# Key selection of a sparse-attention layer: two of six query blocks counted by a compare with sum on VectorE, and masks written into the score tiles

## Chip, core and metric

The kernel runs on one NeuronCore of a Trainium2 chip. A core has five engines that run side by side, each with its own queue of instructions: TensorE (matrix products into PSUM), VectorE, ScalarE and GpSimd (element-wise work and reductions), and SyncE, which here only starts DMAs. The metric is the device time of one execution in microseconds (us), median of several runs; lower is better.

## What is computed

One layer of a decoder trunk over 1024 positions of width 1024, in float32: a half-step SwiGLU feed-forward, then two token mixers side by side (sparse attention A and stick-breaking attention B), each gated and merged, then a second half-step feed-forward. The change lies in the selection of keys for the sparse attention. For each query, an indexer scores all keys up to its own position, and only the 256 best take part in the attention:

```python
dots = einsum('bthd,bsd->bths', qi, k_idx)
score = einsum('bths,bth->bts', relu(dots), wi)
score = where(causal, score, -inf)
_, idx = lax.top_k(score, top_k)            # top_k = 256
valid = idx <= t_pos
# logits of q_a with the chosen keys, softmax, product with the chosen values
```

Queries are handled in blocks of 128. Block i sees (i + 1) x 128 keys. Blocks 0 and 1 have at most 256 keys, so all of them are chosen; blocks 2 to 7 need a selection. What the selection hands on is a mask per block: 0 for a chosen key, -1e30 for any other, to be added to the logits.

## The kernel before

**Stages.** The first feed-forward comes first (to about 640 us in the profile), then the projections of the mixers, the mixers themselves (about 700 to 1425 us), then the output projection and the second feed-forward. Within the mixers the kernel is a set of Python generators. Each `yield` names an engine and the tiles or marks that the next piece of work needs; a planner (`Weave`, lines 94 to 242) holds a model of when each engine is free and each tile ready, and always continues the generator whose next piece can start earliest. Ties go by a rank (0 first), then by the time at which a piece became ready plus an optional slack (the `2.0` in `yield ACT, cand, score[i], 2.0`). The order that comes out is fixed when the program is built: on the chip each engine works through its queue in that order.

**Generators around the change.**

- `indexer` and `dot_out` (1603 to 1642) build the score tiles `score[i]`, float32, 128 queries x (i + 1) x 128 keys, named `u` in the profile, in the order 5, 4, 2, 7, 6, 3. `score_out` sets keys after the query's position to -3e38.
- `topk` (1225 to 1323) makes the selection, once for the group (5, 4, 2) and once for (7, 6, 3). Both run at the same time as everything below.
- `sticks`, `sigmoids`, `stick` (1691 to 1736) and `values` (1792 to 1819) are the stick-breaking attention: a product into PSUM (`psz`), two sigmoids on ScalarE, a scan (line 1701, tile `left`) and a multiplication (1704) on VectorE, transposes on TensorE (`pstT`), a copy on ScalarE (1748) and a subtraction on VectorE (1750) that split the result into a high and a low part (`pt`), and the product with the values (`psy`), which `y_out` stores (`yl`, `yh`).
- `fillers` (1197 to 1222) has the lowest rank: projections (`psf`) of queries, keys, values and gates, which TensorE takes whenever nothing else is ready. Once "gates" is marked, the next fillers are the output projections in `outputs` (2061), first `psob`. These need the marks "gates" and "o", the operands `ybh` and `ybl` in the place of the tiles that the gate projections read, and the mark "c".
- `values` marks "o" at its end, waits for "top0" and "top1", closes the memory of the selection (`chosen.close()`, `keep.close()`: the score tiles among it), and starts `sparse` (1831), which reuses that memory for the loads `uvraw` and marks "c".
- `logits`, `soft`, `latent_values` (1873 to 1967) are the sparse attention proper. Logits (`psL`) start at the mark "sparse", after the last stick; for blocks 5 and 4 the masks need "top0", for 7, 6 and 3 "top1".

**How the selection works.** The 256th largest score is found bit by bit. `count(0.0)` counts the scores that are at least zero, which gives `sig`: +1 if the threshold is positive, -1 if not. Then `by_sign` goes through 31 bits from the highest down. For each bit VectorE sets the bit in a candidate (`cand`, line 1257), ScalarE computes for each block of the group the sign of `sig * score + cand` with the sum over the keys (line 1260; the instruction is followed by a read of its accumulator), VectorE compares the three sums with `thr` (1264, `m`) and keeps the bit or not (1265). `cand` carries the sign bit, so the sum tells how many scores lie above the candidate. Candidates of the next bit need the test of this one; a group's bits are a chain through both engines.

After the bits a few small operations and one more `count(fix)` round the threshold (lines 1271 to 1294). Then each block gets its mask, one block after another: sign of the score against the threshold on ScalarE (1305, `gt`), equality (1308), a running sum for ties (1311, `cum`), the difference (1314), the mask in bfloat16 (1318), and a DMA from GpSimd's queue (1321) to the buffer `bd` in DRAM. The three temporary tiles come from a ring of three (`x2`). The mask is written over the tile `cum`, which is given back only when that DMA has landed; the next block's pass needs all three tiles.

Of the kernel before, what the change touches and what calls it, by code (L numbers as in the profile page):

```python
# [10 lines left out]
F32 = mybir.dt.float32  # L11
F32R = mybir.dt.float32r
I32 = mybir.dt.int32
BF16 = mybir.dt.bfloat16
# [3 lines left out]
ALU = mybir.AluOpType  # L18
# [5 lines left out]
P = 128  # L24
# [221 lines left out]
def trunk(ctx, tc, x, positions, g_ffn1, w1_gate, w1_up, w1_down, g_mix, w_in, g_cq, w_uq_a, w_q_idx,  # L246
# [781 lines left out]
    with ctxf, fp as fpool, psm as psum, tc.manual_schedule(  # L1028
# [193 lines left out]
            mark("gates", *outs)  # L1222


        def topk(group, gi):
            n = len(group)

# [18 lines left out]
            nc.vector.tensor_scalar(kth, sig, TOPK - 0.5, 0.5, op0=ALU.mult, op1=ALU.add)  # L1246
            for b, i in enumerate(group):
                c = slice(b, b + 1)
                nc.vector.tensor_scalar(thr[:, c], sig[:, c], 2 * TOPK - 1.0 - (i + 1) * P, 1.0, op0=ALU.mult, op1=ALU.add)


            def by_sign(bits):

                yield DVE
                nc.vector.tensor_scalar(T, T, -2147483648, None, op0=ALU.bitwise_or)
                for bit in bits:
                    nc.vector.tensor_scalar(cand, T, 1 << bit, None, op0=ALU.bitwise_or)  # L1257
                    for b, i in enumerate(group):
                        yield ACT, cand, score[i], 2.0
                        nc.scalar.activation(junks[1][:, 0:(i + 1) * P], score[i], AF.Sign,  # L1260
                                             scale=sig[:, b:b + 1], bias=cand.bitcast(F32)[:, b:b + 1],
                                             accum_out=cnt[:, b:b + 1])
                    yield DVE, cnt
                    nc.vector.tensor_tensor(m, cnt, thr, op=ALU.is_ge)
                    nc.vector.scalar_tensor_tensor(T, m, bit, T, op0=ALU.logical_shift_left, op1=ALU.bitwise_or)
                nc.vector.tensor_scalar(T, T, 0x7FFFFFFF, None, op0=ALU.bitwise_and)

            nc.vector.memset(T, 0)
            yield from by_sign(range(30, -1, -1))

            lo16, hi16 = tl("lo16", I32), tl("hi16", I32)
            nc.vector.tensor_scalar(lo16, T, 0xFFFF, None, op0=ALU.bitwise_and)
# [24 lines left out]
            for b, i in enumerate(group):  # L1297
                nk = (i + 1) * P
                x2 = here["x2"]
                yield ACT, (x2, 3), fix  # L1300
                tiles = [x2(n_) for n_ in ("eq", "cum", "gt")]
                eq, cum, gt = (t[:, 0:nk] for t in tiles)
                c = slice(b, b + 1)

                nc.scalar.activation(gt, score[i], AF.Sign, bias=fix[:, c], accum_out=cnt[:, c])
                yield DVE, gt

                nc.vector.tensor_scalar(eq, gt, 0.0, STEP, op0=ALU.is_equal, op1=ALU.mult)
                nc.vector.tensor_scalar(rem[:, c], cnt[:, c], -0.5 * STEP, (TOPK - 0.5 * nk) * STEP, op0=ALU.mult, op1=ALU.add)
                yield DVE  # L1310
                nc.vector.tensor_tensor_scan(cum, eq, eq, 0.0, op0=ALU.add, op1=ALU.bypass)
                yield DVE
                nc.vector.scalar_tensor_tensor(rem[:, c], cum[:, nk - 1:nk], 0.5, rem[:, c], op0=ALU.mult, op1=ALU.add)
                nc.vector.tensor_sub(eq, cum, gt)
                give(tiles[2])
                bias = tiles[1].bitcast(BF16)[:, 0:nk]
                yield DVE
                nc.vector.tensor_scalar(bias, eq, rem[:, c], NEG, op0=ALU.is_gt, op1=ALU.mult)
                give(tiles[0])
                yield POOL, tiles[1]  # L1320
                put_low(bd[:, boff[i]:boff[i] + nk], bias)
                give(tiles[1])
            mark(f"top{gi}", bd)

        def heads():
# [923 lines left out]
```

## Time and profile before

| | |
|---|---|
| Time, median of 3 runs (lowest to highest) | 2187.26 us (2185.01 to 2187.8) |
| The profiled execution | 2190.85 us, span 2189.1 us |
| Busy in the span: TensorE / VectorE / ScalarE / GpSimd | 2139.3 / 1550.2 / 1117.2 / 888.5 us |
| Instructions | 30352 |
| Signs of the bit search (line 1260) | 186, 183.4 us of ScalarE, from 808.5 to 1196.3 us, and as many accumulator reads |

Times in the profile are from the start of the span. PE is TensorE's matrix products, PEld its weight loads, DVE is VectorE, ACT ScalarE, POOL GpSimd, SP SyncE. A line number is the line of the kernel; work done in a helper stands under the helper's line, so tiles tell more than lines there. In a group, the number after x is its count, then come the busy time, the mean of one in ns, and the idle time of the engine just before, with what ended it. The clock is the share of TensorE's full clock that was granted. A busy TensorE is not a TensorE at its peak: matmuls overlap in the records.

### The profile page before, as it was taken

To read this page: it belongs to the slowest core of one execution; us is meant where nothing else is said; L and a number is where in the kernel's file an instruction comes from. 1 tells how busy PE (TensorE), PEld (TensorE's weight loads), DVE (VectorE), ACT (ScalarE), POOL (GpSimd) and SP (SyncE) were. 2 spreads that over 40 slices of the span, in tenths; PEclk is the share of its full clock that TensorE was granted. 3 is DMA by queue.
4 is the path that set the end of the run, shared out by engine and by line. 5 is a ranking of instruction groups with operands and counts; after the bars stand their busy time and mean duration, and the time that the engine had idled before them with its cause. 6 is when DMAs were issued, how large, how long until landed. Compare 5 with 4: busy or idle time off the path is not lost.

```text
span 2189.1 us, 30352 instructions
## 1 busy us (share of the span) xinstructions
PE 2139.3 (98%) x10308; PEld 1782.2 (81%) x10308; DVE 1550.2 (71%) x2562; ACT 1117.2 (51%) x2185; POOL 888.5 (41%) x718
## 2 busy tenths in 40 slices
PE   7999999999999999999999899999999999999999
PEld 6888888887889988788888688878888888888887
DVE  7766767678874698677788888853674655678685
ACT  6433333334454358999988565534433232233443
POOL 5555555522354444211111232255465554552223
PEclk9999999999999999999999899999999999999999
DMA  5587878496675353655554433566132332349755
GB/s 156 143 248 209 252 200 255 159 318 230 218 198 169 121 144 127 238 143 176 155 174 140 151 124 107 191 219 219 58 125 92 99 109 92 116 167 322 234 176 188
DMA packets 269053, 381.00 MB, mean 174 GB/s; under 512 B 23265, under 2 KB 157041, under 8 KB 268897
## 3 DMA queue, kind: packets, MB, share of 16 engines
q1 hardware_dynamic: 256384, 339.17, 49.4%
q0 software_dynamic: 12512, 39.89, 5.1%
q8 instruction: 81, 1.33, 0.3%
q14 instruction: 76, 0.61, 0.1%
HBM read 259.94 MB, written 119.05 MB: 173 GB/s over the span
## 4 chain that ended last, share of the span: by engine, by line
PE 53%; issue 9%; DVE 9%; ACT 4%; DMA 4%; POOL 2%; SPq 0%; POOLq 0%; DVEq 0%; ACTq 0%
PE p L737 4%; PE p L738 4%; PE p L736 4%; ACT junka L1260 2%; PE pa L499 2%; PE pa L498 2%; PE pa L497 2%; PE pc L498 2%; PE pc L499 2%; PE pc L497 2%; PE pd L498 2%; PE pd L499 2%; PE pd L497 2%; PE psf L308 2%; PE psf L309 2%
## 5 line engine op out<-in xcount | busy, mean ns | idle before, releaser
L1260 ACT ACTIVATE junka<-u,cand,sig 128x768 bf16<-128x768 f32 (+4 forms) x186 | 183.4, 986 | 7.9 <-DVE cand L1257 6.1
L859 ACT ACTIVATE swh<-swr 128x512 fp32r<-128x512 f32 x48 | 30.2, 629 | 116.8 <-PE pc L499 51.4
L1701 DVE TENSOR_TENSOR_SCAN left<-left 128x640 f32<-128x640 f32 (+3 forms) x64 | 86.1, 1348 | 3.1 <-ACT left L1693 2.9
L1194 POOL DMA_DIRECT2D gd<-evg x32 | 18.0, 563 | 140.9 <-ACT evg L1189 124.6
L860 DVE TENSOR_TENSOR swr<-swr,swh 128x512 f32<-128x512 f32 x48 | 42.0, 875 | 38.1 <-ACT swh L859 35.2
L1750 DVE TENSOR_TENSOR pt<-pstT,pt 128x512 fp32r<-128x512 f32 (+1 forms) x96 | 51.0, 550 | 24.3 <-ACT pt L1748 23.7
L640 ACT ACTIVATE b0u<-b0u 128x512 f32<-128x512 f32 x20 | 12.7, 633 | 99.0 <-DVE b0u L520 83.0
L1750 DVE TENSOR_TENSOR pt<-pspT,pt 128x512 fp32r<-128x512 f32 x72 | 46.4, 683 | 19.0 <-ACT pt L1748 18.9
L1748 ACT ACTIVATE pt<-pspT 128x512 fp32r<-128x512 f32 x72 | 39.6, 596 | 33.6 <-PE pspT L1960 33.5
L1881 ACT ACTIVATE e<-e,nm 128x768 f32<-128x768 f32 (+7 forms) x64 | 49.4, 775 | 11.4 <-DVE nm L1876 10.9
L737 PE MATMUL p<-aT,aS 128*128 128x512 f32 x132 | 51.9, 394 | 2.4 <-DVE aT L378 2.3
L1614 DVE SCALAR_TENSOR_TENSOR u<-relu,WI,u 128x512 f32<-128x512 f32 (+1 forms) x70 | 50.2, 739 | 5.3 <-ACT relu L1607 4.3
L1869 DVE CUSTOM_DVE_ANT_0 e<-psL,bias 128x512 f32<-128x512 f32 (+3 forms) x96 | 49.7, 549 | 5.1 <-PE psL L1906 5.1
L737 PE MATMUL p<-bT,bS 128*128 128x512 f32 x132 | 51.5, 390 | 0.4 <-DVE bT L378 0.4
L1704 DVE TENSOR_TENSOR sa<-sa,left 128x639 f32<-128x639 f32 (+3 forms) x64 | 48.0, 753 | 4.0 <-ACT sa L1695 0.2
L738 PE MATMUL p<-aT,aS 128*128 128x512 f32 x132 | 50.7, 389 | 0.0
L738 PE MATMUL p<-bT,bS 128*128 128x512 f32 x132 | 50.4, 389 | 0.0
L1607 ACT ACTIVATE relu<-psdot 128x512 f32<-128x512 f32 (+1 forms) x80 | 39.7, 522 | 20.7 <-DVE u L1614 9.2
L1960 PE MATMUL pspT<-ident,e 128*128 128x128 f32 x288 | 41.7, 287 | 7.8 <-DVE e L1884 7.7
L1748 ACT ACTIVATE pt<-pstT 128x512 fp32r<-128x512 f32 (+1 forms) x96 | 46.3, 502 | 3.7 <-PE pstT L1804 3.6
L1960 PEld LDWEIGHTS pspT<-ident,e 128*128 128x128 f32 x288 | 36.2, 148 | 14.0 <-DVE e L1884 9.0
L1695 ACT ACTIVATE sa<-psz 128x512 f32<-128x512 f32 (+2 forms) x96 | 47.0, 509 | 0.1
(3038 smaller groups left out, 8257.1 us busy)
## 6 DMA issues: line engine op xcount, KB each, us to landing
aw<-in_w_down_dram SPq DMA_DIRECT2D x33, 512.0 KB, 5.2
bw<-in_w_down_dram SPq DMA_DIRECT2D x33, 512.0 KB, 5.0
swr<-in_w_in_dram SPq DMA_DIRECT2D x48, 256.0 KB, 6.2
a0r<-in_w_gate_dram SPq DMA_DIRECT2D x22, 512.0 KB, 7.5
a1r<-in_w_up_dram SPq DMA_DIRECT2D x22, 512.0 KB, 7.4
b0r<-in_w_gate_dram SPq DMA_DIRECT2D x22, 512.0 KB, 4.0
b1r<-in_w_up_dram SPq DMA_DIRECT2D x22, 512.0 KB, 3.8
x<-in_x_dram SPq DMA_DIRECT2D x16, 512.0 KB, 6.9
```

Source lines behind the costliest of these rows:

```text
L497: nc.tensor.matmul(ps, a[:, c], b[k][:, HI], start=start and k == 0, stop=False, skip_group_check=True)
L498: nc.tensor.matmul(ps, a[:, c], b[k][:, LO], start=False, stop=False, skip_group_check=True)
L499: ins = nc.tensor.matmul(ps, a[:, l], b[k][:, HI], start=False, stop=k == 3, skip_group_check=True)
L736: nc.tensor.matmul(ps[q][m], S[:, h], T[:, HI], start=p == 0, stop=False)
L737: nc.tensor.matmul(ps[q][m], S[:, h], T[:, LO], start=False, stop=False)
L738: nc.tensor.matmul(ps[q][m], S[:, l], T[:, HI], start=False, stop=p == last)
L1260: nc.scalar.activation(junks[1][:, 0:(i + 1) * P], score[i], AF.Sign, scale=sig[:, b:b + 1], bias=cand.bitcast(F32)[:, b:b + 1], accum_out ...
L1614: nc.vector.scalar_tensor_tensor(ac, r, wv, ac, op0=ALU.mult, op1=ALU.add)
L1701: nc.vector.tensor_tensor_scan(back, back, back, 1.0, op0=ALU.mult, op1=ALU.bypass)
L1748: nc.scalar.activation(pt[:, off:512], tp[:, off:512], AF.Copy)
L1750: nc.vector.tensor_sub(pt[:, 512 + off:1024], tp[:, off:512], f32(pt[:, off:512]))
L1960: nc.tensor.transpose(tp[:, q * P:(q + 1) * P], E[n + q][:, j * P:(j + 1) * P], ident)
```

## The change

Blocks 2 and 3, one in each group, are counted in another way. For these two, `flip` multiplies the score tile in place by `-sig` before the bits and again after them (which restores it). In each bit their count is then a comparison on VectorE, `score < cand`, with its sum over the keys, in the form that `count` has already; the other two blocks of a group keep their sign on ScalarE. The comparison of a group is issued ahead of its signs. `thr` for these blocks is set for a plain count in place of a sum of signs. In the mask passes of all six blocks the temporary tile `cum` is given back once it has been read, and the mask is written into the block's own score tile, from which the DMA to `bd` reads it.

```diff
+        compared = (3, 2)
+
         def topk(group, gi):
...
-                nc.vector.tensor_scalar(thr[:, c], sig[:, c], 2 * TOPK - 1.0 - (i + 1) * P, 1.0, op0=ALU.mult, op1=ALU.add)
+                nk = (i + 1) * P
+                if i in compared:
+                    nc.vector.tensor_scalar(thr[:, c], sig[:, c], TOPK - 0.5 * (nk + 1), 0.5 * (nk + 1), op0=ALU.mult, op1=ALU.add)
+                else:
+                    nc.vector.tensor_scalar(thr[:, c], sig[:, c], 2 * TOPK - 1.0 - nk, 1.0, op0=ALU.mult, op1=ALU.add)
+
+            def flip():
+
+                for b, i in enumerate(group):
+                    if i in compared:
+                        yield DVE
+                        nc.vector.tensor_scalar(score[i], score[i], sig[:, b:b + 1], -1.0, op0=ALU.mult, op1=ALU.mult)
...
-                    for b, i in enumerate(group):
+                    for b, i in sorted(enumerate(group), key=lambda bi: bi[1] not in compared):
+                        if i in compared:
+                            yield DVE, cand, score[i], 2.0
+                            nc.vector.tensor_scalar(junks[0][:, 0:(i + 1) * P], score[i], cand.bitcast(F32)[:, b:b + 1], 0.0,
+                                                    op0=ALU.is_lt, op1=ALU.add, accum_out=cnt[:, b:b + 1])
+                            continue
                         yield ACT, cand, score[i], 2.0
                         nc.scalar.activation(junks[1][:, 0:(i + 1) * P], score[i], AF.Sign,
...
             nc.vector.memset(T, 0)
+            yield from flip()
             yield from by_sign(range(30, -1, -1))
+            yield from flip()
...
                 nc.vector.tensor_sub(eq, cum, gt)
                 give(tiles[2])
-                bias = tiles[1].bitcast(BF16)[:, 0:nk]
+                give(tiles[1])
+                bias = score[i].bitcast(BF16)[:, 0:nk]
                 yield DVE
                 nc.vector.tensor_scalar(bias, eq, rem[:, c], NEG, op0=ALU.is_gt, op1=ALU.mult)
                 give(tiles[0])
-                yield POOL, tiles[1]
+                yield POOL, score[i]
                 put_low(bd[:, boff[i]:boff[i] + nk], bias)
-                give(tiles[1])
```

## The prediction

> **What bounds the kernel now.** I read the page's busy table first, then the busy time in stretches of 50 us, then the groups and single rows around the key selection. The columns of the stretches are: from:to, length, then busy time (instructions) of TensorE, its weight loads, VectorE, ScalarE and GpSimd, the granted clock, the DMA share and GB/s.
>
> ```profile
> PE 2139.3 (98%) x10308; PEld 1782.2 (81%) x10308; DVE 1550.2 (71%) x2562; ACT 1117.2 (51%) x2185; POOL 888.5 (41%) x718
> ...
> 800.00:850.00 50.00, 47.67 (x250) 40.93 (x249) 44.37 (x86) 38.85 (x80) 20.50 (x21) 0.97 0.33 107
> ...
> 1000.00:1050.00 50.00, 49.56 (x264) 40.44 (x264) 36.94 (x74) 49.77 (x116) 4.40 (x9) 1.00 0.61 170
> 1050.00:1100.00 50.00, 49.48 (x258) 39.93 (x257) 38.16 (x66) 49.21 (x110) 7.59 (x14) 1.00 0.55 161
> ...
> 1200.00:1250.00 50.00, 39.70 (x169) 29.66 (x168) 42.41 (x117) 23.90 (x45) 14.44 (x17) 0.83 0.46 159
> 1250.00:1300.00 50.00, 49.52 (x280) 42.56 (x279) 40.59 (x153) 30.93 (x79) 17.28 (x17) 1.00 0.41 130
> ...
> 1950.00:2000.00 50.00, 50.00 (x223) 41.40 (x222) 44.98 (x58) 19.44 (x35) 19.35 (x12) 1.00 0.84 291
> ...
> 800.00:1205.00 405.00, 397.23 (x2084) 328.12 (x2083) 320.38 (x636) 373.33 (x810) 83.17 (x120) 1.00 0.53 162
> ...
> 1205.00:1253.00 48.00, 37.88 (x162) 28.39 (x161) 40.25 (x118) 24.37 (x45) 11.60 (x14) 0.82 0.46 158
> ```
>
> TensorE is busy for 98% of the span. The change touches no matmul, so it can win only time in which TensorE stands idle or runs at a lowered clock. ScalarE is full from 1000 to 1100 (49.8 and 49.2 of 50), yet TensorE is 99% busy there too: the planner fills it with the gate projections (`fillers`). So a shorter ScalarE queue gives no direct gain in that stage. The one large hole lies behind it: from 1205 to 1253 TensorE is busy 37.9 of 48 us, at a clock of 0.82. That is 10.1 us idle and about 0.18 x 37.9 = 6.8 us of slow clock: **16.9 us is what can be won here**.
>
> Why the hole is there is read from single rows (columns: start, length, engine, line; in brackets the idle time before and what ended it), from three one-line summaries, and from the landing line of the mask buffer `bd`.
>
> ```profile
> L1189 ACT ACTIVATE evg<-psf x32: 574/596/677, 936.8 to 1215.3; 128x512 f32<-128x512 f32 x32
> ...
> L1701 DVE TENSOR_TENSOR_SCAN left<-left x64: 416/1349/2292, 912.6 to 1188.4; 128x640 f32<-128x640 f32 x8, 128x768 f32<-128x768 f32 x8, 128x896 f32<-128x896 f32 x8, 128x1024 f32<-128x1024 f32 x8
> ...
> 1206.65 0.59 ACT L1757 ACTIVATE yl<-psy 64x512 f32<-64x512 f32 x1 [6.69 <-DMA ybld<-yl]
> ...
> 1208.37 0.32 SPq L2068 DMA_DIRECT2D ybh<-ybhd  x1
> ...
> 1210.62 1.14 ACT L1305 ACTIVATE gt<-u,fix 128x1024 f16<-128x1024 f32 x1
> ...
> 1220.36 0.47 PE L1960 MATMUL pspT<-ident,e 128*128 128x128 f32 x1 [4.42 <-DVE e L1884]
> ...
> 1221.01 0.32 SPq L2069 DMA_DIRECT2D ybl<-ybld  x1
> ...
> 1224.35 1.03 ACT L1305 ACTIVATE gt<-u,fix 128x896 f16<-128x896 f32 x1
> ...
> 1228.52 2.02 DVE L1311 TENSOR_TENSOR_SCAN cum<-eq 128x896 f16<-128x896 f16 x1 [2.56 <-DMA bd<-cum]
> ...
> 1237.43 0.71 ACT L1305 ACTIVATE gt<-u,fix 128x512 f16<-128x512 f32 x1
> ...
> 1245.08 0.57 POOL L1321 DMA_DIRECT2D bd<-cum  x1 [7.44 <-DVE ri L1883]
> ...
> 1247.40 0.98 POOL L1840 MEMSET uvraw<- 128x512 f32 x2 [1.74 <-DMA bd<-cum]
> ...
> 1250.79 0.39 PE L308 MATMUL psob<-ybh,ob0h 128*128 128x512 f32 x1
> ...
> DMA to landing us min/median/max: 1.9/2.6/5.4
> ```
>
> The gate projections end at about 1215 (last eviction of `psf` at 1215.3). The next filler, the projection `psob`, begins only at 1250.8. In between TensorE has the attention work alone and waits for VectorE (4.42 us before 1220.36). `psob` needs the mark "c", which `values` gives after "top0" and "top1", once the tiles of the selection can be closed. The `uvraw` memset at 1247.4, the first work on the freed memory, waits for the last mask DMA. So **the selection of the second group (blocks 7, 6, 3) decides when the hole ends**: its last sign is at 1196.3 (below), its three mask passes begin at 1210.6, 1224.4 and 1237.4, and its last mask leaves at 1245.1. The stick-breaking work was done by then: last scan at 1188.4, last `yl` at 1206.7.
>
> **The change, part by part.** First the price of what moves: signs on ScalarE with their accumulator reads (groups between 900 and 1200; busy, mean ns), then compares with sum on VectorE.
>
> ```profile
> L1260 ACT ACTIVATE junka<-u,cand,sig x186: 692/1016/1376, 808.5 to 1196.3; 128x768 bf16<-128x768 f32 x31, 128x640 bf16<-128x640 f32 x31, 128x384 bf16<-128x384 f32 x31, 128x1024 bf16<-128x1024 f32 x31
> ...
> L1260 ACT ACTIVATION_READ_ACCUMULATOR junka<-u,cand,sig 128x1 f32 x138 | 29.2, 211 | 0.0
> ...
> L1260 ACT ACTIVATE junka<-u,cand,sig 128x512 bf16<-128x512 f32 x29 | 23.9, 825 | 0.3
> ...
> L1260 ACT ACTIVATE junka<-u,cand,sig 128x384 bf16<-128x384 f32 x18 | 13.2, 734 | 0.1
> ...
> L1237 DVE TENSOR_SCALAR_CACHE_REDUCE junkv<-u x6: 544/878/1208, 800.2 to 873.6; 128x768 bf16<-128x768 f32 x1, 128x640 bf16<-128x640 f32 x1, 128x384 bf16<-128x384 f32 x1, 128x1024 bf16<-128x1024 f32 x1
> ...
> L1237 DVE TENSOR_SCALAR_CACHE_REDUCE junkv<-u,fix 128x768 bf16<-128x768 f32 x1 | 1.0, 1005 | 0.0
> ...
> L1237 DVE TENSOR_SCALAR_CACHE_REDUCE junkv<-u,fix 128x384 bf16<-128x384 f32 x1 | 0.6, 606 | 0.0
> ...
> 1207.88 0.73 DVE L1237 TENSOR_SCALAR_CACHE_REDUCE junkv<-u,fix 128x512 bf16<-128x512 f32 x1
> 1208.54 0.07 DVE L1237 DVE_READ_ACCUMULATOR junkv<-u,fix 128x1 f32 x1
> ...
> L1884 DVE TENSOR_SCALAR e<-e,ri 128x768 f32<-128x768 f32 x8 | 5.5, 685 | 0.3
> ```
>
> 1. *Signs removed.* 31 bits for block 2 (384 keys) and 31 for block 3 (512 keys): 31 x (0.734 + 0.211) + 31 x (0.825 + 0.211) = 29.3 + 32.1 = 61.4 us of ScalarE. From 800 to 1205 ScalarE falls from 373.3 to about 312 of 405 us (77%).
>
> 2. *Compares added.* 31 x (0.606 + 0.07) + 31 x (0.73 + 0.07) = 21.0 + 24.8 = 45.8 us of VectorE. The changed line has the same operation with the same shapes as L1237, so I take those rows. The four flips are VectorE scalings in place; each is shorter than the 768-element one of L1884 (0.685 us), so 2.7 us at most, once per block before and after all bits. VectorE rises from 320.4 to 320.4 + 45.8 + 2.7 = 369 of 405 us (91%).
>
> The 768-element pair bounds this from below: a scaling without a sum takes 0.685 us where the compare with sum takes 1.005 us, so at the scaling's pace the 45.8 us would be some 31. The Trainium skill ("VectorE: DVE Perf Modes", the perf-mode tier table) gives fp32 `tensor_scalar` from SBUF two elements a cycle; by its breakdown of 150 cycles and half a cycle per element an estimate for both kinds of compare together is 26 us, before their reads. The row with the sum, 1.005 us for 768, shows no such rate, and the row decides.
>
> 3. *What the bits gain.* The second group's 31 bits run from about 875 (its first counts end at 874) to 1196.3, 10.4 us a bit, of which its own three signs (median 1.016) and reads (0.211) are only some 3.7 us; the rest is standing in a full ScalarE queue three times a bit. One of three stands goes away; the compare takes one on VectorE instead, issued ahead of the two signs. If a third of a bit is saved and a quarter of that is given back, a bit is 2.6 us shorter and the second group ends 31 x 2.6 = 80 us earlier. To be out of the way at 1206.7 (`yl`, end of the sticks) it needs to end some 35 us earlier. I take that as reached, since the margin is double; the bounds are nothing and 80.
>
> 4. *Masks into the score tiles.* `cum` is no longer held by the DMA. The visible wait for that is 2.56 us (VectorE before 1228.5), and the planner spaces the passes 13 us apart because it reckons with the landing. On their own the masks would end some 2 x 2.6 to 2 x 5.4 us earlier, 5 to 11 us, by the landing line. Behind step 3 this is off the path. The DMA itself, its bytes and its place in GpSimd's queue stay; the score tile is held to its landing instead, and it was held to the same mark before.
>
> 5. *What is late next.* With "top1" early, "c" follows the end of the values, about 1213 as I estimate it (the `yl` of 1206.65 and its way into DRAM). Then `psob` waits for its operands: the `ybh`/`ybl` loads take the place of `h2`, so they start only as the gate projections end; the last is issued at 1221.0 and lands some 5 us later. So `psob` can begin at about 1226 instead of 1250.8, and the hole shrinks from 1215-1251 to 1215-1226, 11 of 36 us: 16.9 x 11/36 = 5.2 us stay and **11.7 us are won**. Three mask passes less in that stretch relieve VectorE, which had 40.3 of 48 us there; I count nothing for it.
>
> 6. *What VectorE costs the stage before.* The end of the sticks is now set by ScalarE (92% from 800 to 1205) and would be set by VectorE at 91%. The highest share of VectorE in any stretch is 44.98 of 50, 90%. At 90% the 369 us need 410 us, 5 later than now; at 95% they need 388, 17 earlier. I take 0 to 1 us lost, since the fillers cover TensorE on either side.
>
> Sum: -11.7 + 0.7 = **-11.0 us**. The profiled execution took 2190.85 us, 1.75 us around its span of 2189.1, so it would be 2179.9. It lies 3.6 us above the median of the runs, 2187.26, so I put the time at 2176.3, rounded **2176**.
>
> **The rivals.** Two waits of VectorE over 800 to 1205 matter for them (us, times, longest):
>
> ```profile
> DVE m L1264 <- ACT junka L1260: 25.4, 23, 2.6
> DVE pt L1750 <- ACT pt L1748: 23.7, 28, 2.2
> ```
>
> *A. The whole hole closes.* ScalarE's relief ends the sticks before the gate projections are used up, and these fill TensorE until `psob` is ready. Condition: VectorE keeps up at about 95%. For it: those waits for ScalarE, 49 us, shrink when ScalarE has room. Against it: no stretch shows VectorE above 90%. Time: nearly all of 16.9 us and some of the 2.3 us idle from 800 to 850, about -18 us: 2169.
>
> *B. The bits come no faster.* The compare stands as long in VectorE's queue as the sign stood in ScalarE's, and the second sign is issued only after it. Then "top1" stays near 1245 but for the DMA wait, 3 us or so are won and VectorE gives them back: 2186. For it: VectorE is at 91%. Against it: two of three stands remain on an engine that has gone from 92% to 77%.
>
> *C. Slower: VectorE becomes the bound.* A compare of 0.6 to 0.8 us stands in front of the scans (L1701) and of the split subtraction L1750, whose `pt` frees the two transpose banks; and the test `m` still waits for the last sign with all this behind it. If half of the 45.8 us lengthens the stage because the 49 us of waits stay, the sticks end at 1228 with the fillers gone at about 1215; 23 us are lost and step 5's 11.7 won: 2187 + 11 = 2198. It decides from the point at which the sticks end 12 us later than now; with the whole 45.8 us it would be 2221. The Trainium skill ("TensorE: Matmul & The Clock Gate", engine queue depths) says that ScalarE's and VectorE's queues are strictly first in, first out. The 25.4 us of waits before `m` agree with that as far as a wait can; by that rule alone C's mechanism holds, and only its size is open.
>
> **How the numbers follow.** Forecast 0.45 (own range 2170 to 2182), A 0.20, B 0.15, C 0.20. Within 0.2%, 4.4 us, which is about what a measurement of this kernel can tell from no change, lie B and little else. So faster 0.65, same 0.16, slower 0.19. The range goes from 2165 (A with a few us more, the lower bound on the compares) to 2195 (B and the milder half of C); about 0.2 is left out, mostly C.
>
> **What would show it.** Right: 124 signs at the sign's line and 62 compares of 0.61 and 0.73 us; ScalarE near 310 and VectorE near 365 us from 800 to 1205; the last sign before 1165; `uvraw` waiting for no mask DMA; `psob` from about 1226; TensorE above 44 of 50 us from 1200 to 1250 with a clock above 0.9. Wrong: a last stick scan after 1200 (C), a last sign after 1185 (B), no gap between the gates and `psob` (A), or new idle time of TensorE from 800 to 1200.

## The result and the profile after

| | before | after |
|---|---|---|
| Time, median of 7 runs each (lowest to highest) | 2187.8 us (2185.01 to 2193.09) | 2176.9 us (2172.76 to 2181.68) |
| Ratio to before, 95% interval | 1 | 0.9945 (0.9928 to 0.9962) |
| The profiled execution | 2190.85 us, span 2189.1 us | 2175.96 us, span 2174.2 us |

The changed kernel is 0.55% faster; the forecast was 2176. In the table of experiments below, one run of first_before (2421.5 us) and one of yl_on_pool (9050.66 us) were slow ones: they count in the medians of their rows and not in the ratios. The page of the changed kernel, the line of busy times:

```profile
PE 2133.8 (98%) x10308; PEld 1779.0 (82%) x10308; DVE 1583.0 (73%) x2690; ACT 1072.8 (49%) x2061; POOL 885.4 (41%) x716
```

The same stretches of the changed kernel as were shown of before, with the same columns (length, busy time of TensorE, weight loads, VectorE, ScalarE, GpSimd, then the clock):

```profile
950.00:1000.00 50.00, 50.00 (x263) 41.06 (x262) 46.18 (x95) 46.70 (x102) 7.75 (x14) 1.00 0.57 165
1000.00:1050.00 50.00, 50.00 (x275) 41.05 (x274) 46.18 (x98) 49.22 (x108) 4.41 (x8) 1.00 0.58 157
1050.00:1100.00 50.00, 50.00 (x255) 41.09 (x255) 45.57 (x102) 40.21 (x86) 8.39 (x15) 1.00 0.57 170
...
1200.00:1250.00 50.00, 43.57 (x222) 34.40 (x222) 43.91 (x139) 31.27 (x62) 13.39 (x17) 0.97 0.50 172
1250.00:1300.00 50.00, 47.78 (x266) 40.70 (x265) 44.03 (x151) 31.74 (x78) 11.76 (x11) 0.97 0.30 95
...
800.00:1205.00 405.00, 400.15 (x2099) 330.75 (x2097) 362.25 (x783) 333.92 (x693) 84.89 (x124) 1.00 0.54 168
...
1205.00:1253.00 48.00, 42.41 (x222) 33.93 (x223) 41.95 (x135) 28.81 (x58) 12.35 (x17) 0.96 0.42 142
```

TensorE from 1205 to 1253 went from 37.88 us at a clock of 0.82 to 42.41 us at 0.96. What is lost there is the length less busy time times clock: 48 - 42.41 x 0.96 = 7.3 us, against 16.9. So 9.6 us were won where 11.7 were forecast. From 800 to 1205 TensorE is busy 2.9 us more than before, with VectorE at 92% in the stretches from 950 to 1050. From 1250 to 1300 a little is given back.

What answers to the single rows of before (summaries by line, then rows of the timeline: start, length, engine, line; in brackets the idle time before and what ended it):

```profile
L1278 ACT ACTIVATE junka<-u,cand,sig x124: 912/1116/1349, 811.4 to 1160.4; 128x768 bf16<-128x768 f32 x31, 128x640 bf16<-128x640 f32 x31, 128x1024 bf16<-128x1024 f32 x31, 128x896 bf16<-128x896 f32 x31
...
L1274 DVE TENSOR_SCALAR_CACHE_REDUCE junkv<-u,cand x62: 585/666/747, 812.5 to 1160.2; 128x384 bf16<-128x384 f32 x31, 128x512 bf16<-128x512 f32 x31
...
L1262 DVE TENSOR_SCALAR u<-u,sig x4: 415/447/481, 804.8 to 1168.9; 128x384 f32<-128x384 f32 x2, 128x512 f32<-128x512 f32 x2
...
L1721 DVE TENSOR_TENSOR_SCAN left<-left x64: 391/1346/2285, 915.8 to 1187.4; 128x640 f32<-128x640 f32 x8, 128x768 f32<-128x768 f32 x8, 128x896 f32<-128x896 f32 x8, 128x1024 f32<-128x1024 f32 x8
...
L1189 ACT ACTIVATE evg<-psf x32: 573/598/712, 925.0 to 1203.9; 128x512 f32<-128x512 f32 x32
```

```profile
1181.87 1.14 ACT L1325 ACTIVATE gt<-u,fix 128x1024 f16<-128x1024 f32 x1
...
1199.98 0.71 ACT L1325 ACTIVATE gt<-u,fix 128x512 f16<-128x512 f32 x1
...
1207.35 0.54 POOL L1342 DMA_DIRECT2D bd<-u  x1
...
1207.50 0.58 PE L1925 MATMUL psL<-kkh,qs 128*128 128x256 f32 x1 [3.33 <-DVE mx L1889]
...
1213.62 0.32 SPq L2089 DMA_DIRECT2D ybl<-ybld  x1
...
1213.68 0.99 POOL L1860 MEMSET uvraw<- 128x512 f32 x2 [5.26 <-DMA bd<-u]
...
1229.16 0.40 PE L308 MATMUL psob<-ybh,ob0h 128*128 128x512 f32 x1
```

The last sign comes at 1160.4 instead of 1196.3, 36 us earlier. The three mask passes of the second group begin at 1181.9 to 1200.0 (1210.6 to 1237.4 before), the last mask leaves at 1207.35 (1245.1), `uvraw` starts at 1213.7 (1247.4), and `psob` follows at 1229.2 (1250.8). The last stick scan has not moved: 1187.4 against 1188.4. The gate projections end 11 us earlier, so the hole also begins earlier, at 1203.

The waits of VectorE in the changed kernel from 800 to 1205 (us, times, longest):

```profile
DVE pt L1770 <- ACT pt L1768: 11.6, 24, 1.4
DVE m L1282 <- ACT junka L1278: 7.5, 11, 1.5
```

The two waits for ScalarE that stood at 23.7 and 25.4 us are 11.6 and 7.5 us now. These 30 us less of waiting are where most of VectorE's 41.9 us of extra busy time went.

### The profile page after: what moved, and what is told of

The parts are those of the page before. It is cut to its first block, busy times and chain, and to the rows that moved or that the text cites. A ratio compares the mean times of both kernels' runs of the same rounds, so it can differ in the third digit from the quotient of the medians.

```text
span 2174.2 us, 30345 instructions
## 1 busy us (share of the span) xinstructions
PE 2133.8 (98%) x10308; PEld 1779.0 (82%) x10308; DVE 1583.0 (73%) x2690; ACT 1072.8 (49%) x2061; POOL 885.4 (41%) x716
## 5 line engine op out<-in xcount | busy, mean ns | idle before, releaser
L1278 ACT ACTIVATE junka<-u,cand,sig 128x768 bf16<-128x768 f32 (+1 forms) x124 | 135.5, 1093 | 3.0 <-DVE cand L1270 1.8
L860 DVE TENSOR_TENSOR swr<-swr,swh 128x512 f32<-128x512 f32 x48 | 43.2, 900 | 41.6 <-ACT swh L859 36.6
L1770 DVE TENSOR_TENSOR pt<-pstT,pt 128x512 fp32r<-128x512 f32 (+1 forms) x96 | 51.5, 551 | 12.9 <-ACT pt L1768 11.6
L1768 ACT ACTIVATE pt<-pspT 128x512 fp32r<-128x512 f32 x72 | 39.2, 595 | 29.1 <-PE pspT L1980 28.9
L1627 ACT ACTIVATE relu<-psdot 128x512 f32<-128x512 f32 (+1 forms) x80 | 39.8, 521 | 25.4 <-DVE u L1634 17.4
L1713 ACT ACTIVATE left<-psz 128x512 f32<-128x512 f32 (+2 forms) x96 | 47.1, 506 | 6.5 <-PE psz L1748 3.6
L2043 POOL TENSOR_TENSOR o<-o,gate 128x512 f32<-128x512 f32 x16 | 21.8, 1361 | 66.2 <-ACT o L2038 66.2
```

The costliest lines, as they stand in the source:

```text
L1768: nc.scalar.activation(pt[:, off:512], tp[:, off:512], AF.Copy)
L1770: nc.vector.tensor_sub(pt[:, 512 + off:1024], tp[:, off:512], f32(pt[:, off:512]))
```

## The experiments

All of them are the changed kernel with the edit shown, except "first_before", which is the kernel before with an edit. Two measures serve for every run. **Lost in the hole**: from the last matmul of the gate projections to the first of `psob`, length less busy time times clock. **Lost behind**: the same from there to the output projection `psm`. Each is from the one execution that was profiled, so differences of 2 or 3 us in them mean little.

| kernel | median us | ratio to before (95%) | last sign | last scan | gates end | `psob` | lost in the hole | lost behind |
|---|---|---|---|---|---|---|---|---|
| before | | 1 | 1196.3 | 1188.4 | 1214.1 | 1250.8 | 16.2 | 5.1 |
| after | 2176.9 | 0.9945 (0.9928 to 0.9962) | 1160.4 | 1187.4 | 1202.6 | 1229.2 | 7.6 | 5.4 |
| masks_only | 2190.35 | 1.0006 (0.9997 to 1.0015) | 1194.6 | 1181.4 | 1210.5 | 1235.5 | 12.0 | 11.5 |
| compares_only | 2182.4 | 0.9971 (0.9959 to 0.9983) | 1159.6 | 1191.5 | 1201.8 | 1228.0 | 7.7 | 9.3 |
| only3 | 2178.37 | 0.9950 (0.9938 to 0.9963) | 1163.9 | 1190.9 | 1206.1 | 1232.4 | 7.3 | 3.7 |
| only2 | 2179.83 | 0.9960 (0.9948 to 0.9973) | 1173.4 | 1188.2 | 1211.2 | 1226.9 | 6.6 | 9.5 |
| late_bits | 2180.77 | 0.9965 (0.9954 to 0.9976) | 1187.7 | 1148.5 | 1204.2 | 1227.2 | 10.6 | 9.6 |
| first_before | 2243.36 | 1.0239 (1.0218 to 1.0259) | 1089.8 | 1260.0 | 1251.0 | 1292.7 | 11.3 | 11.4 |
| twice | 2209.78 | 1.0095 (1.0080 to 1.0110) | 1220.3 | 1164.8 | 1200.8 | 1262.4 | 42.4 | 5.3 |
| signs_first | 2197.84 | 1.0043 (1.0028 to 1.0058) | 1134.8 | 1199.4 | 1192.2 | 1238.9 | 12.9 | 17.9 |
| narrow | 2179.64 | 0.9960 (0.9938 to 0.9982) | 1137.0 | 1183.7 | 1212.6 | 1231.9 | 1.7 | 15.7 |
| added | 2203.78 | 1.0054 (1.0034 to 1.0074) | 1224.4 | 1190.3 | 1213.4 | 1265.2 | 25.0 | 7.0 |
| first_group5 | 2195.99 | 1.0028 (1.0017 to 1.0040) | 1213.2 | 1164.4 | 1215.4 | 1251.7 | 17.3 | 16.4 |
| yl_on_pool | 2184.17 | 0.9972 (0.9960 to 0.9984) | 1161.3 | 1198.7 | 1202.7 | 1232.2 | 10.5 | 8.2 |

The rows by which the last two columns can be followed, for before and for after, hole first:

```profile
1214.40:1250.80 36.40, 26.28 (x108) 18.70 (x107) 29.51 (x78) 18.09 (x35) 9.30 (x10) 0.77 0.44 151
1250.80:1432.00 181.20, 176.15 (x959) 149.50 (x958) 145.70 (x422) 104.82 (x225) 55.46 (x51) 1.00 0.43 142
```

```profile
1202.90:1229.20 26.30, 19.87 (x96) 14.28 (x95) 23.36 (x76) 16.56 (x31) 7.71 (x10) 0.94 0.61 217
1229.20:1415.00 185.80, 182.21 (x988) 154.57 (x986) 150.43 (x433) 107.11 (x232) 53.23 (x48) 0.99 0.40 131
```

36.4 - 26.28 x 0.77 = 16.2 us and 26.3 - 19.87 x 0.94 = 7.6 us: 8.6 us won in the hole; behind it 5.1 and 5.4, no change.

### Each half of the change alone

**masks_only** leaves all counts on ScalarE and keeps the masks in the score tiles:

```diff
-        compared = (3, 2)
+        compared = ()
```

> The changed kernel with no block compared on VectorE: only the masks go into the score tiles. Theory (the selection ends earlier because its bits come faster, so the output projections start earlier): the last sign stays near 1196 us, the three mask passes of the second group shorten by 5 to 11 us, the first matmul of psob comes near 1242 instead of 1250.8, and the time is 2 to 5 us below before, about 2184. Rival 1 (the masks carry the gain, since a pass no longer waits for the DMA of the one before): nearly the whole 11 us, about 2177. Rival 2 (the relief of ScalarE carries it): no difference from before, 2187.

**compares_only** keeps the compares and holds the mask over `cum` until its DMA has landed, as before:

```diff
-                give(tiles[1])
-                bias = score[i].bitcast(BF16)[:, 0:nk]
+                bias = tiles[1].bitcast(BF16)[:, 0:nk]
...
-                yield POOL, score[i]
+                yield POOL, tiles[1]
                 put_low(bd[:, boff[i]:boff[i] + nk], bias)
+                give(tiles[1])
```

> The changed kernel with the mask written over cum and held until its DMA has landed, as before; blocks 3 and 2 still compared on VectorE. Theory: last sign near 1160, the mask passes of the second group take some 5 to 11 us more than in the changed kernel, psob between 1230 and 1240, time 2177 to 2181. Rival 1 (masks): near 2187. Rival 2 (ScalarE's relief): 2177, the same as the changed kernel, with psob wherever it may be.

The hole and what lies behind it, in masks_only and then in compares_only:

```profile
1210.80:1235.50 24.70, 16.03 (x65) 11.03 (x64) 23.69 (x59) 11.46 (x24) 7.53 (x9) 0.79 0.50 181
1235.50:1430.00 194.50, 186.74 (x1000) 157.24 (x998) 152.43 (x441) 110.70 (x237) 55.49 (x52) 0.98 0.42 135
```

```profile
1202.00:1228.00 26.00, 21.08 (x88) 14.15 (x87) 21.57 (x73) 16.07 (x29) 6.83 (x10) 0.87 0.58 196
1228.00:1421.00 193.00, 185.59 (x1000) 156.16 (x998) 153.52 (x440) 110.21 (x237) 54.65 (x50) 0.99 0.41 133
```

The masks alone bring nothing (1.0006). They do what they should in their place: the last mask leaves at 1232.2 instead of 1245.1, and 4 us less are lost in the hole. (From the last sign to the last mask it is 11 us less; the last sign itself is 1.7 us earlier.) But 6 us more are lost behind it. I had expected 2184 and missed, because I stopped counting at `psob`.

The time of the compares alone lies 1 us above the range expected (2177 to 2181), and their `psob` begins 2 us ahead of the earliest expected (1230). They close the hole as far as the whole change does, 7.7 against 7.6 us, although their last mask leaves 11 us later, at 1218.1: with the compares `psob` does not wait for the masks. What the whole change has beyond them, 0.9945 against 0.9971, lies behind the hole (5.4 against 9.3 us). The two intervals just overlap, so this part of the gain is likely rather than certain.

### One block at a time

**only3** and **only2** count one block by a compare:

```diff
-        compared = (3, 2)
+        compared = (3,)
```

```diff
-        compared = (3, 2)
+        compared = (2,)
```

> Only block 3, of the second group, is compared on VectorE; block 2 keeps its sign; masks in the score tiles. VectorE gets about 25 us instead of 46, ScalarE loses about 32 instead of 61. Theory: the second group's chain is the one that counts; it still has only two signs a bit, so its last sign comes near 1170, psob near 1232 and the time is 2177 to 2181. Rival 2 (ScalarE's relief in proportion): half of the gain, about 2182. If the balance of the two engines sets the end of the sticks, this one ends them some 5 us earlier than the changed kernel and is as fast or faster: 2172 to 2177.

> Only block 2, of the first group, is compared on VectorE; the second group keeps three signs a bit. Theory: the second group gains only through a less crowded ScalarE, its last sign comes near 1180 and its masks end near 1222, psob near 1235, the time 2179 to 2184: less than block 3 alone. Rival 2 (ScalarE's relief in proportion): half of the gain, about 2182, the same as block 3 alone.

Both times came as expected, though the `psob` of only2 began 8 us before the hour expected for it. Block 3 alone, in the second group, has the whole gain within the intervals. Block 2 alone, which touches only the first group, has most of it: its last sign is 23 us earlier than before, I take it because the second group's signs stand behind fewer others. The parts do not add up. Once the selection is some 20 us earlier, something else sets `psob`.

### Does the order of the pieces do it alone?

**first_before** is the kernel before with its signs put ahead of all other work of ScalarE by the planner's slack:

```diff
-                        yield ACT, cand, score[i], 2.0
+                        yield ACT, cand, score[i], -8.0
```

> The kernel before (all three blocks by sign, masks over cum) with the slack of the signs at -8 instead of 2, so that the planner prefers them among equal ranks; no work is moved to VectorE. Theory: the last sign comes near 1150 to 1165, the second group's masks end before 1215, psob comes before 1235 and the time is 2178 to 2184, without any relief of ScalarE; the sticks may end some us later, since ScalarE is as full as before. Rival 2: no better than before, 2187 or more.

**late_bits** lets signs and compares stand back:

```diff
-                            yield DVE, cand, score[i], 2.0
+                            yield DVE, cand, score[i], 12.0
...
-                        yield ACT, cand, score[i], 2.0
+                        yield ACT, cand, score[i], 12.0
```

> The changed kernel with the slack of signs and compares at 12 instead of 2, so that the planner lets other work go first and the bits come later; all work the same. Theory (an early end of the selection is what wins): the last sign comes after 1185, the second group's masks end after 1230, psob after 1240, and most of the gain is lost: 2184 to 2190. Rival 2 (the relief of ScalarE in the stage before wins, whenever the selection ends): 2173 to 2178, as the changed kernel, perhaps better because the sticks go first.

**signs_first** issues the signs of a bit ahead of its compare:

```diff
-                    for b, i in sorted(enumerate(group), key=lambda bi: bi[1] not in compared):
+                    for b, i in sorted(enumerate(group), key=lambda bi: bi[1] in compared):
```

> The changed kernel with the two signs of a bit issued ahead of the compare, instead of behind it. If a sign's wait for the compare's place in VectorE's queue is a part of a bit's length, the last sign comes 10 to 20 us earlier than 1160; by the theory psob then comes only as early as the loads of ybh and ybl allow, near 1229 as before, so the time stays within 3 us of the changed kernel, 2174 to 2180. If an earlier selection always pays, it is 2170 or less.

**first_group5** lets the second group alone stand back:

```diff
-                            yield DVE, cand, score[i], 2.0
+                            yield DVE, cand, score[i], (2.0, 5.0)[gi]
...
-                        yield ACT, cand, score[i], 2.0
+                        yield ACT, cand, score[i], (2.0, 5.0)[gi]
```

> The changed kernel with the slack of signs and compares at 5 for the second group and 2 for the first. Slack 12 for both let the sticks end 39 us earlier but held the first group's masks, and with them the first logits, until 1190. Here the first group's masks should come as early as in the changed kernel (before 1120), the sticks end some 10 us earlier than 1187, and the logits start while the gates still fill TensorE: the hole loses 4 to 8 us, 2169 to 2174. If what counts is only the later of the two ends, sticks or selection, it stays at 2176 to 2182.

None of the four came out by its theory, and only in first_before does the rival ("no better than before") hold. They say most. A stretch of first_before, from 907 us on, where the products of the sticks (`psz`) begin in the kernel before; here they begin at 948:

```profile
907.00:948.00 41.00, 22.83 (x83) 17.68 (x82) 12.19 (x51) 39.20 (x75) 6.31 (x9) 0.75 0.42 128
```

With the signs first, the selection is done 107 us earlier (last sign at 1089.8), and the kernel is 2.4% slower: ScalarE, at 39.2 of 41 us, is taken from the copies for which TensorE stands (22.8 of 41 us busy, at a clock of 0.75; between 800 and 950 it waits 18.2 us for `evl`, which is made from ScalarE's `evh`), and the last scan of the sticks slips to 1260.0. Both chains draw on ScalarE. To favour the one is to delay the other, and `psob` comes only after both. In signs_first it is the same on a smaller scale. Its row of `uvraw`:

```profile
1220.68 0.98 POOL L1860 MEMSET uvraw<- 128x512 f32 x2 [2.16 <-DMA ybld<-yl]
```

Now the wait is for the sticks' last output, `ybld<-yl`, and no longer for a mask; the selection is 26 us earlier than in the changed kernel, the last scan is 12 us later, and the gates are used up at 1192. In first_group5 the opposite:

```profile
1215.60:1251.70 36.10, 24.76 (x98) 17.72 (x97) 33.21 (x94) 15.43 (x31) 6.20 (x8) 0.76 0.33 126
...
1250.33 0.99 POOL L1860 MEMSET uvraw<- 128x512 f32 x2 [1.71 <-DMA bd<-u]
```

The same instructions as in the changed kernel, sticks that end 23 us earlier, and the whole gain is gone: the second group's last mask lands at 1250, `psob` starts at 1251.7, and the hole is that of before, 17.3 us. (11 us more than in the changed kernel are lost behind it too, so not all of the 19 us between the medians is the hole's.) This is the cleanest evidence that **the end of the second group's selection is what the change has to move**. The planner's order differs as well, so other effects of the order are not excluded by this run alone. late_bits lies between: sticks 39 us earlier, last mask issued at 1223.9, `psob` at 1227.2, just after `uvraw` (1227.0); its interval overlaps that of the changed kernel. There an `uvraw` 13 us later costs `psob` nothing, which fits compares_only.

### What a compare costs

**twice** issues each compare two times:

```diff
+                            yield DVE, cand, score[i], 2.0
+                            nc.vector.tensor_scalar(junks[0][:, 0:(i + 1) * P], score[i], cand.bitcast(F32)[:, b:b + 1], 0.0,
+                                                    op0=ALU.is_lt, op1=ALU.add, accum_out=cnt[:, b:b + 1])
                             yield DVE, cand, score[i], 2.0
```

> The changed kernel with each of the 62 compares issued twice: about 46 us more of VectorE between 800 and 1205, which would have 408 of 405 us to do. If VectorE is the bound of the stage (rival C of the prediction, from this load on), the last scan moves from 1187 to 1225 or later, the gates run out before it and the time is 2195 to 2215. If VectorE still hides behind ScalarE and TensorE, it stays within 5 us of the changed kernel, 2175 to 2182.

**added** keeps all 186 signs of the kernel before and issues the 62 compares besides, with their sums unused (in each bit the sign of block 2 or 3 then stands first):

```diff
-                if i in compared:
+                if False:
...
-                                                    op0=ALU.is_lt, op1=ALU.add, accum_out=cnt[:, b:b + 1])
-                            continue
+                                                    op0=ALU.is_lt, op1=ALU.add, accum_out=m.bitcast(F32)[:, b:b + 1])
...
-            yield from flip()
             yield from by_sign(range(30, -1, -1))
-            yield from flip()
```

> All 186 signs stay on ScalarE and decide; the 62 compares of blocks 3 and 2 are done besides, their sums unused; masks in the score tiles. ScalarE has 373 of 405 us as before, VectorE about 365. Against the kernel with the masks alone (1.0006 of before) this is the price of the compares without any relief. If VectorE has room beside a full ScalarE: 2187 to 2194. If each bit stands once more in VectorE's queue and that counts: last sign after 1210, psob after 1255 and 2200 to 2220.

**narrow** compares only the first 8 keys and leaves the other keys of blocks 2 and 3 out of the bit search:

```diff
-                            nc.vector.tensor_scalar(junks[0][:, 0:(i + 1) * P], score[i], cand.bitcast(F32)[:, b:b + 1], 0.0,
+                            nc.vector.tensor_scalar(junks[0][:, 0:8], score[i][:, 0:8], cand.bitcast(F32)[:, b:b + 1], 0.0,
```

> The changed kernel with the 62 compares over the first 8 keys only; the other keys of blocks 3 and 2 are left out of the bit search. ScalarE's relief is whole, VectorE gets some 15 us instead of 46. If the relief of ScalarE is what wins and VectorE's compares give a part back, it is clearly below the changed kernel: 2160 to 2172, with the mark c (the uvraw memset) before 1205 and the last scan before 1180. If the compares are hidden, it is 2174 to 2179, the same as the changed kernel.

The stretches of twice, then of added (800 to 1205 first, the hole behind it):

```profile
800.00:1205.00 405.00, 397.21 (x2099) 329.60 (x2097) 374.56 (x823) 320.69 (x668) 87.22 (x123) 1.00 0.54 166
...
1201.00:1262.40 61.40, 29.71 (x106) 19.84 (x104) 53.70 (x173) 34.85 (x63) 7.81 (x12) 0.64 0.29 109
```

```profile
800.00:1205.00 405.00, 397.00 (x2084) 325.35 (x2083) 345.83 (x743) 366.22 (x793) 82.76 (x120) 1.00 0.53 160
1205.00:1253.00 48.00, 35.09 (x149) 25.74 (x147) 39.17 (x121) 30.49 (x60) 7.16 (x10) 0.82 0.40 142
```

A second set of compares makes the changed kernel 33 us slower, and 35 us more are lost in the hole: VectorE's load shows up as a later *selection* (last sign 1220.3), not as later sticks (last scan 1164.8). In added the compares, put beside the unchanged signs, cost 0.5% against masks_only (1.0054 against 1.0006), again through the selection (last sign 1224.4, 30 us later, with the last scan at 1190.3). So a compare is not free: in added 62 of them delay the second group's end by 30 us, about 1 us for each of its 31 bits, and in twice a second 62 delay it by 60 us. Taking the signs away gains more than the first 62 cost: from added to after the last sign comes 64 us earlier, 2.1 us a bit.

The rows of narrow: the hole and behind it, the memset of `uvraw`, and TensorE's waits from 1362 to 1436; last, the same waits of the changed kernel:

```profile
1212.90:1231.90 19.00, 17.34 (x97) 13.58 (x97) 17.90 (x47) 12.53 (x26) 4.07 (x3) 1.00 0.62 239
1231.90:1421.00 189.10, 176.95 (x947) 149.43 (x945) 138.52 (x409) 101.47 (x220) 53.83 (x48) 0.98 0.39 129
```

```profile
1202.50 1.24 POOL L1860 MEMSET uvraw<- 128x512 f32 x2 [2.55 <-DMA ybld<-yl]
```

```profile
PE psya L308 <- DVE o L2052: 3.6, 2, 2.5
PE psya L308 <- DVE yal L2021: 2.7, 2, 1.7
PE psm L308 <- DVE o L2052: 2.6, 1, 2.6
```

```profile
PE psm L308 <- DVE o L2052: 0.9, 1, 0.9
PE psya L308 <- DVE yal L2021: 0.5, 2, 0.2
```

With nearly free compares the hole is all but closed: 1.7 us lost, at a full clock. By the hole alone that is 6 us better than the changed kernel; yet the time is 2179.64, no better. 15.7 us are lost behind, where the projections `psya` and `psm` wait for the merges `o` and the splits `yal` on VectorE, 8.9 us in these three rows, where the changed kernel has 1.4.

In the column "lost behind", the runs fall into three groups by when the last matmul of `psob` comes against that of the logits (`psL`). Where it comes 17 to 19 us ahead of them (before, after, only3, twice, added), 4 to 7 us are lost behind the hole. Where it comes 32 or 33 us ahead (masks_only, compares_only, only2, late_bits, first_before, yl_on_pool), 8 to 12. Where it comes 4 us after them (signs_first, narrow, first_group5), 16 to 18. The planner chooses this order anew for each kernel. No run set it by itself, so that this order causes the loss is a reading and not shown.

### A version that might be faster

VectorE is at 362 of 405 us and GpSimd at 85, so **yl_on_pool** moves one of the split subtractions of the sticks:

```diff
-            yield DVE, yl, yh
-            nc.vector.tensor_tensor(yl[0:HD], yt, f32(yh[0:HD]), op=ALU.subtract)
+            yield POOL, yl, yh
+            nc.gpsimd.tensor_tensor(yl[0:HD], yt, f32(yh[0:HD]), op=ALU.subtract)
```

> The changed kernel with one more edit: the subtraction that makes the low part of each stick-breaking output (line 1788, 16 times 0.68 us on VectorE) goes to GpSimd, which has 85 of 405 us to do in that stage. VectorE gets back some 11 of its 46 us. If VectorE's load is what still delays the selection, as the run with narrow compares suggests (c at 1202 instead of 1214), c comes between 1205 and 1212 and the hole between the gates and psob loses 2 to 5 us: 2170 to 2175, provided the idle time in the last 40 us of the attention stays below 5 us as in the changed kernel. If the fillers are used up earlier and that stretch opens as it did with narrow compares, it stays at 2175 to 2181.

It is 7 us above the changed kernel in the medians, and the two intervals only just overlap, so it is likely slower. Its stage from 800 to 1205, then four rows of its timeline:

```profile
800.00:1205.00 405.00, 400.52 (x2097) 330.87 (x2095) 364.82 (x766) 332.10 (x690) 107.77 (x139) 1.00 0.54 165
```

```profile
964.77 3.84 DVE L1721 TENSOR_TENSOR_SCAN left<-left 128x1024 f32<-128x1024 f32 x1
965.13 1.31 POOL L1788 TENSOR_TENSOR yl<-yl,yh 64x512 fp32r<-64x512 f32 x1
...
1066.55 2.28 DVE L1721 TENSOR_TENSOR_SCAN left<-left 128x1024 f32<-128x1024 f32 x1
1066.98 3.99 POOL L1788 TENSOR_TENSOR yl<-yl,yh 64x512 fp32r<-64x512 f32 x1
```

The subtractions left VectorE (15 of the 16 lie in this stretch, 11.3 us in the changed kernel), and its busy time did not fall: 364.8 against 362.3 us. The last scan is 11 us later (1198.7). The two summaries of the scans from 800 to 1215, in the changed kernel and in this one (forms and count, then busy us and mean ns):

```profile
L1721 DVE TENSOR_TENSOR_SCAN left<-left 128x640 f32<-128x640 f32 (+3 forms) x64 | 85.8, 1347 | 1.1 <-ACT left L1713 1.1
```

```profile
L1721 DVE TENSOR_TENSOR_SCAN left<-left 128x640 f32<-128x640 f32 (+3 forms) x64 | 91.1, 1429 | 1.0 <-ACT left L1713 1.0
```

The scans alone take 5.3 us more. Why is taken up at the end. None of the versions tried beats the changed kernel beyond the intervals; only3 equals it with half the edit.

## Why the prediction was right, step by step

The sum was -11.0 us, and the medians differ by 10.9. The mechanism that it named, an earlier end of the second group's selection and with it an earlier `psob`, is the one that the runs show. That the number fits so closely is partly luck: the hole gave less than forecast (9.6 us for 11.7), and the stage before gave 2.9 us where 0.7 were to be lost.

**What can be won** was 16.9 us in the hole. Right in place: 9.6 of the 14.9 us between the two profiled executions lie from 1205 to 1253. TensorE's 2.9 us more of busy time from 800 to 1205 are a second part. The rest is no more than runs of one kernel differ by (8 us from lowest to highest before).

**Step 1, signs.** 124 are left. ScalarE fell to 333.9 us and not to 312. The durations that went add up to about 61 us, as predicted, but the busy time of the whole span fell by only 44.4 (1117.2 to 1072.8): the accumulator reads, 62 x 0.211 = 13 us of the sum, overlap the instructions beside them in the records. A sum of durations is not a sum of busy time. Nothing hung on that term.

**Step 2, compares.** 62, from 0.585 to 0.747 us in the two sizes; predicted were 0.606 and 0.73. The flips took 0.415 to 0.481 us, 1.8 us in all, within the bound of 2.7. VectorE stands at 362.3 us, predicted 369. The 62 compares took 41.6 us before their reads, where the prediction's estimate from the Trainium skill ("VectorE: DVE Perf Modes", the perf-mode tier table) was 26 us; worked out again from the same breakdown, that estimate is 24 to 25 us. The Trainium skill ("SBUF — State Buffer", "Who interferes with whom") excludes from the two-port modes the form of `tensor_scalar` that also writes out its accumulator; the compares' 0.585 us at the least agree with that, against my estimate from the table.

**Step 3, the bits.** Right in sign, and the condition of 35 us was just met (36), but the margin that I called double was not there: 36 us over 31 bits are 1.2 us a bit, not 2.6. The step had a third of a bit saved, 3.5 us, and a quarter of that, 0.9 us, given back on VectorE. By added the part given back is about 1 us a bit, so that part was right in size. By the step from added to after the saving is 2.1 us a bit: this is the term that was too large, by two thirds. Why one sign of three saves less than a third of a bit was not tested. Nor were 35 us needed: in only2 the last sign is 23 us earlier, and `psob` begins at 1226.9.

**Step 4, masks.** In the hole the step holds. compares_only loses the same 7.7 us there with its masks 11 us later, and masks_only gains 4 us where I had said 5 to 11 us for the masks themselves (11 were measured from last sign to last mask). What it missed is that masks also change the order behind `psob`: alone they lose there what they win, and on top of the compares they may win some 5 us.

**Step 5, what is late next.** `psob` began at 1229.2, predicted 1226, and the last `ybl` load left at 1213.6 rather than 1221. The wait that the step named does not show. In the changed kernel the last load waits for the last output of the sticks (`ybld<-yl`) and not for the gate projections, and it lands 3.6 us after its issue, 12 us before `psob`. In the kernel before it landed 7.0 us after 1221.0, 23 us before `psob`. In both, the first matmul of `psob` shows no idle time before it: it stands in TensorE's queue behind logits and products of the sparse attention, and these wait for VectorE. The longest wait of TensorE in the changed kernel from 1202.9 to 1229.2 (us, times, longest):

```profile
PE psL L1925 <- DVE mx L1889: 5.0, 4, 3.3
```

So neither "c" nor the loads hold `psob` up on the chip; they can only set the place that the planner gives it. By the planner's own model, computed while the program is built, "c" comes last in the kernel before and the landing of the last `ybl` load comes last in the changed kernel, which is the step's account; no trace shows that model. As a time on the chip, 1226 was near by luck. "c" followed the last mask (5.26 us of waiting for `bd`) and not the values, at 1213.7, near the 1213 that I had estimated for the values: the hour was right by coincidence, the row that I had named as a sign was not there. That this wait was not the last to end is shown by compares_only and late_bits, where `uvraw` starts 7 and 13 us later and `psob` no later.

**Step 6, the stage before.** 0 to 1 us of loss was predicted, and 2.9 us were won: the small idle times of TensorE between 950 and 1100 are gone (0.96 us of them from 1000 to 1100). The remark that a shorter ScalarE queue gives no direct gain there was slightly wrong. VectorE stood at 92% for 100 us, above the 90% at which I had drawn the line.

**The rivals.** A, the whole hole closing, did not come; in narrow the hole all but closed, and the kernel was no faster, since what was won there was lost behind it. B is refuted by the last sign, 36 us earlier. C's mechanism exists and has the price of the upper cases (twice, 33 us), but it acts through the selection instead of the sticks, and with one set of compares the relief of ScalarE outweighs it. Of the signs of being right, three did not come: ScalarE near 310 us (333.9), `uvraw` waiting for no mask, and TensorE above 44 us from 1200 to 1250 (43.6).

## What to carry to other kernels

When two chains share an engine and one wait joins them, ask which chain ends last and what the engine's relief does to that one; moving priority between them (first_before, signs_first, first_group5) only swaps which is late. Price work that goes to the other engine in the chain in which it stands, not by that engine's share of busy time. And before a hole is counted as won, look at the work that filled time behind it: narrow closed the hole and gained nothing.

## What the runs showed of the hardware

In yl_on_pool VectorE and GpSimd held each other up. There a scan of 1024 elements that takes 2.28 us took 3.84 us when a GpSimd subtraction of 1.31 us began 0.36 us after it, 1.56 us longer. In the second pair of rows the subtraction took 3.99 us beside a scan of 2.28 us: it ended 2.14 us after the scan, more than its usual whole length, so it had done nothing before the scan was over. The trace goes on: a VectorE multiplication with two inputs (line 1724, 1.06 us) came next, and the test `m` behind it, 0.155 us in the median, took 1.24 us and ended with the subtraction, at 1070.98 and 1070.97. So the hold-up reaches the chain of the bits too. The Trainium skill ("SBUF — State Buffer", "Who interferes with whom") says that a VectorE instruction with two inputs in SBUF and a GpSimd instruction that reads SBUF exclude each other, and that the second waits for the whole of the first. The second pair agrees with that. The first agrees in its size, but there the instruction that lengthened is the one that shows the earlier start; the profile's starts are not exact enough to say which was served first.
